# Attention's value projections held until the sixth and seventh stretch of the recurrence have gone by

## The chip, the core and the metric

The kernel runs on one NeuronCore of a Trainium2 chip. The metric is device time in microseconds (us), the median of several executions. One further execution was recorded by the hardware profiler; its trace is what is read below. Engines are named as in the profile: PE (TensorE matmul), PEld (its weight load), DVE (VectorE), ACT (ScalarE), POOL (GpSimd), SP (SyncE, which here only issues DMAs; ACT issues some too).

## The reference

Two layers are computed one after the other on 1024 tokens of width 1024. The change lies in the second one, whose token mixer runs two branches on the same normalised input and joins them:

```python
h = _rmsnorm(x, mix_norm_gain[l])
proj = h @ w_in[l]
p_rwkv, p_attn = proj[..., :RWKV_COLS], proj[..., RWKV_COLS:]
# branch 1: a recurrence over tokens, 8 heads of 64
def step(state, inp):
    r_t, w_t, k_t, v_t, kk_t, a_t = inp
    sa = jnp.einsum('bhvk,bhk->bhv', state, -kk_t)
    state = (state * w_t[:, :, None, :] + sa[..., None] * (kk_t * a_t)[:, :, None, :]
             + v_t[..., None] * k_t[:, :, None, :])
    y = jnp.einsum('bhvk,bhk->bhv', state, r_t)
    return state, y
# branch 2: causal attention, 8 heads of 64, with rotary positions on part of q and k
q, k, v = three slices of p_attn, 512 columns each
```

(The line on q, k and v stands for a few lines of the reference.) The two branches' outputs are normalised, gated, concatenated and projected; a feed-forward layer follows.

## The kernel before

**The recurrence.** The 1024 tokens are cut into 8 stretches of 128 (`NU` = 8, numbered u = 0 to 7 here; the sixth and the seventh are u = 5 and u = 6), each of 4 chunks of 32. For a stretch, `rwkv_unit` makes products on PE, then solves a triangular system in 31 steps on POOL (tiles `fs`, `Z`, `M`), after which `Z` goes through DRAM (`dz`) into the tile `xt`, of which there is one. `rwkv_maps` turns that into four maps `A` (lines 1479 and 1496, with additions on DVE). `rwkv_chain` then takes 4 steps in sequence, c0 to c3: 8 matmuls (line 1524), a multiplication on DVE that gives the next state `ST`, and a copy on ACT of the outputs into `yv`. After the fourth step `yv` goes to DRAM (`dyn`). The loop in `rwkv` runs units, maps and chains of consecutive stretches against each other.

**Attention.** `attn_in` projects q, k and v: 3 x 4 projections of 128 columns, each with its own weights of 512 KB. `weights` loads them into a tile `wraw` (two buffers), ACT rounds them to `whi`, DVE takes the rest as `wlo`; both are then used by 48 matmuls (lines 196 to 198: f32 as three products of high and low parts, 8 tiles of the contraction, two halves of the tokens). DVE scales the result into `at`, which goes to DRAM (`dqkv`). I call the four value projections V0 to V3. Below that, `attn_heads` reloads a head's q and k into tiles that share the `wraw`, `whi` and `wlo` buffers, with subtractions on POOL (`qq`, `kl`) and a fill of `qm`; `attn_max` (lines 1751 to 1759) computes a bound on the scores in 12 pairs of matmuls, each reduced on DVE, transposes it and sends it through DRAM (`dmx`) into `qm`; the scores proper (lines 1854, 1855), an exponential on ACT and a gather of values (line 1877) follow. `attn_first` does the heads and maxima of heads 0 and 1 before the attention loop; `rwkv_out` normalises the recurrence's output (`yn`, `gn`, `bon`).

**Order.** A scheduler with a timeline model sorts the instructions of all engines before the kernel is built, within what data and buffers allow; on the chip each engine takes its instructions in that fixed order. Each of SP's and ACT's DMA queues also issues in order, and each DMA waits until the eighth DMA before it, over all queues, has landed. A dependence that is added to the program can thus move instructions on all engines.

Of the kernel before, what the change touches and what calls it, by code (L numbers as in the profile page):

```python
# [17 lines left out]
P = 128  # L18
# [15 lines left out]
NU = T2 // P  # L34
# [14 lines left out]
class Build:  # L49
# [122 lines left out]
            self.ts(hi, src, 1.0, ALU.mult, eng=self.nc.gpsimd)  # L172
        self.tt(lo, src, hi.bitcast(F32), ALU.subtract, eng=lo_eng)

    def weights(self, segs, gain=None):


        kt = max(k + s.shape[0] // P for s, k, _ in segs)
        m = max(c + s.shape[1] for s, _, c in segs)
        raw = self.wp.tile([P, kt, m], F32, tag="wraw", name=self.nm("wraw"))  # L180
        for s, k, c in segs:
            self.dma(out=raw[:, k:k + s.shape[0] // P, c:c + s.shape[1]], in_=s.rearrange("(k p) m -> p k m", p=P))
        if gain is not None:
            self.tt(raw, raw, gain.unsqueeze(2).to_broadcast([P, kt, m]), ALU.mult, eng=self.nc.gpsimd)
        hi = self.wp.tile([P, kt, m], F32R, tag="whi", name=self.nm("whi"))
        lo = self.wp.tile([P, kt, m], F32R, tag="wlo", name=self.nm("wlo"))
        self.split_to(hi, lo, raw)
        return hi, lo

    def wcol(self, src, c0, m, gain=None):  # L190
        return self.weights([(src[:, c0:c0 + m], 0, 0)], gain)

    def mm3(self, ps, a, b, start, stop, **kw):

# [766 lines left out]
    def rows(self, weights, rhs, ch, acc, sink, scale, apart, between={}):  # L961


        tot = {}

        def one(j, w, ch):
            def f(ci, a, b, ps):
                src = sink(j, a, b, ps)
                if j < KD - 2:
                    self.square_acc(acc, src, j, a, b, scale)  # L970
                    return
                if a not in tot:
                    tot[a] = self.sums_ps()
                    self.add_sums(tot[a], acc[:, a:b], True, False)
                self.square_sum(tot[a], src, False, j == KD - 1, scale)

            self.proj(w, rhs, ch, f)

        end = KD - 2 if apart else KD
        for j in range(end):  # L980
            one(j, weights(j), ch)
            if j in between:
                between[j]()
        w = {j: weights(j) for j in range(end, KD)}
        res = []
        for c in ch:
            for j in w:
                one(j, w[j], [c])
            res.append(self.rstd(tot[c[0]], c[1] - c[0], D))
        return res  # L990
# [524 lines left out]
    def rwkv_chain(self, u, maps, wd):  # L1515

        nc = self.nc
        yv = self.small([P, 4, P], tag="yv", bufs=1)
        with self.tc.high_priority():
            for c in range(4):  # L1520
                S, nxt = (self.rwkv_state(4 * u + c + d) for d in range(2))
                ps = self.bank([96, 8, 64], "c0")
                for h in range(8):
                    nc.tensor.matmul(ps[:, h], maps[c][:, h], S[:, h], start=True, stop=True)
                if nxt is not None:
                    self.tt(nxt[:64].rearrange("p (q e) v -> p q e v", q=4), ps[:64].rearrange("p (q e) v -> p q e v", q=4),
                            wd[:, :, c].unsqueeze(3).to_broadcast([64, 4, 2, 64]), ALU.mult)
                nc.scalar.copy(yv[32 * c:32 * c + 32], ps[64:].rearrange("p (q e) v -> p q (e v)", q=4))
                self.rstate.pop(4 * u + c)
        self.dma(out=self.dyn[P * u:P * u + P], in_=yv)  # L1530

    def rwkv(self):

        self.xt = self.small([P, 8, P], tag="xt", bufs=1)
        self.nc.gpsimd.memset(self.xt, 0.0)
        prev = last = None
        for u in range(NU + 1):
            cur = None
            if u < NU:
                if u % 2 == 0:  # L1540
                    sl = self.lora_part(u // 2)
                cur = self.rwkv_unit(u, sl)
            if prev:
                if last:
                    self.rwkv_chain(u - 2, *last)
                last = self.rwkv_maps(prev)
            prev = cur
        self.rwkv_chain(NU - 1, *last)
# [68 lines left out]
    def attn_in(self):  # L1617
        self.dqkv = self.dram([3, 4, P, T2], "dqkv")
        for i in range(3):
            for j in range(4):  # L1620
                w = self.wcol(self.I["w_in_2"][0], 1696 + 512 * i + j * P, P)
                t = self.slot([P, T2], name="at", tag="T")
                self.proj(w, self.x, CH2, lambda ci, a, b, ps: self.tt(t[:, a:b], ps, self.rs[:, a:b], ALU.mult))
                self.dma(out=self.dqkv[i, j], in_=t)
            if i < 2:
                self.rotary(i)
# [542 lines left out]
```

## Time and profile before

| | |
|---|---|
| median of 3 runs | 3237.48 us (3234.71 to 3238.14) |
| the profiled execution | 3233.1 us |
| its span in the trace | 3231.4 us |
| PE busy | 93% of the span |
| DVE, POOL, ACT busy | 62%, 41%, 35% |
| mean granted PE clock | 0.941 |

[...] Times in the rows below are counted from the start of the span.

### The profile page before, as it was taken

How to read it: one execution, taken by the hardware profiler on the slowest of the kernel's cores; microseconds unless marked ns; L12 is line 12 of the kernel's file. 1: busy time of each engine (PE TensorE's matmuls, PEld its weight loads, DVE VectorE, ACT ScalarE, POOL GpSimd, SP SyncE). 2: the span in 40 equal slices, each digit the busy share in tenths (PEclk: the TensorE clock that was granted, in tenths of full speed). 3: DMA queues.
4: the chain of work that ended last, by engine and by line, in shares of the span. 5: the costliest groups of instructions: out<-in, count | busy, mean ns of one | idle time of the engine just before them, and what ended most of it. 6: DMA issues, size and time to landing. Idle time of an engine off the chain costs nothing.

```text
span 3231.4 us, 52682 instructions
## 1 busy us (share of the span) xinstructions
PE 3009.3 (93%) x20614; PEld 2678.5 (83%) x20614; DVE 2009.6 (62%) x3618; ACT 1142.4 (35%) x2168; POOL 1335.0 (41%) x1291
## 2 busy tenths in 40 slices
PE   7999999989799999999999988788988899999998
PEld 6999998979799999877877776677778788887777
DVE  7556654674676666466776555558656766664666
ACT  3344313334343333311333323424444333334111
POOL 3767310033654444232532365543214744454430
PEclk9999999989799999999899989858998899999999
DMA  5333532335222222432223554533425122224321
GB/s 148 86 94 111 174 98 59 105 101 139 78 66 79 81 82 81 150 104 74 90 95 131 146 126 112 137 99 108 115 98 196 53 85 79 80 83 174 113 85 53
DMA packets 322535, 336.83 MB, mean 104 GB/s; under 512 B 60081, under 2 KB 270734, under 8 KB 322286
## 3 DMA queue, kind: packets, MB, share of 16 engines
q1 hardware_dynamic: 289646, 310.38, 31.0%
q10 hardware_dynamic: 32640, 23.08, 2.3%
q8 instruction: 162, 2.65, 0.3%
q14 instruction: 87, 0.71, 0.1%
HBM read 232.66 MB, written 96.40 MB: 102 GB/s over the span
## 4 chain that ended last, share of the span: by engine, by line
PE 61%; DVE 11%; POOL 7%; issue 5%; DMA 4%; ACT 2%; SPq 2%; ACTq 0%; DVEq 0%; POOLq 0%
PE pm L196 13%; PE pm L197 12%; PE pm L198 12%; PE px L197 5%; PE px L196 5%; PE px L198 5%; POOL fs L149 2%; POOL Z L149 2%; DVE dn L149 2%; SPq L142 2%; PE px L292 1%; DVE t L149 1%; PE pa L1877 1%; DMA M<-dm 1%; PE pc L1604 1%
## 5 line engine op out<-in xcount | busy, mean ns | idle before, releaser
L196 PE MATMUL pm<-xh,whi 128*128 128x512 f32 (+5 forms) x1344 | 446.9, 333 | 14.2 <-DVE th L149 11.5
L198 PE MATMUL pm<-xh,wlo 128*128 128x512 f32 (+5 forms) x1344 | 446.8, 333 | 0.0
L197 PE MATMUL pm<-xl,whi 128*128 128x512 f32 (+5 forms) x1344 | 446.4, 332 | 0.0
L149 DVE TENSOR_TENSOR y<-y,pm 128x512 f32<-128x512 f32 (+1 forms) x336 | 218.1, 659 | 159.4 <-PE pm L198 159.1
L196 PE MATMUL pm<-dn,dn 128*128 128x512 f32 (+1 forms) x736 | 286.0, 389 | 6.5 <-DVE y L149 6.2
L196 PEld LDWEIGHTS pm<-xh,whi 128*128 128x128 f32 (+1 forms) x1344 | 257.8, 192 | 35.8 <-DVE th L149 12.4
L197 PE MATMUL pm<-dn,dn 128*128 128x512 f32 (+1 forms) x736 | 282.4, 384 | 1.3 <-POOL dn L149 1.3
L198 PE MATMUL pm<-dn,dn 128*128 128x512 f32 (+1 forms) x736 | 282.5, 384 | 0.0
L197 PEld LDWEIGHTS pm<-xl,whi 128*128 128x128 f32 (+1 forms) x1344 | 257.6, 192 | 19.7 <-issue 0.9
L198 PEld LDWEIGHTS pm<-xh,wlo 128*128 128x128 f32 (+1 forms) x1344 | 257.8, 192 | 19.1 <-issue 0.5
L149 POOL TENSOR_TENSOR dn<-hid,dn 128x1024 fp32r<-128x1024 f32 x44 | 131.8, 3012 | 250.9 <-ACT dn L1161 250.9
L197 PE MATMUL px<-t,sh 128*128 128x258 f32 (+2 forms) x684 | 218.7, 320 | 6.9 <-DVE t L149 6.8
L196 PE MATMUL px<-t,sh 128*128 128x258 f32 (+2 forms) x684 | 217.2, 318 | 0.4 <-DVE gt L149 0.3
L198 PE MATMUL px<-t,sl 128*128 128x258 f32 (+2 forms) x684 | 216.1, 316 | 0.0
L149 DVE TENSOR_TENSOR wlo<-wraw,whi 128x1024 fp32r<-128x1024 f32 (+2 forms) x114 | 153.9, 1351 | 76.2 <-ACT whi L170 74.7
L196 PEld LDWEIGHTS pm<-dn,dn 128*128 128x128 f32 x736 | 138.2, 188 | 43.7 <-DVE y L149 14.2
L170 ACT CAST whi<-wraw 128x1024 fp32r<-128x1024 f32 (+2 forms) x114 | 103.4, 908 | 185.7 <-PE pm L197 154.8
L197 PEld LDWEIGHTS pm<-dn,dn 128*128 128x128 f32 x736 | 138.4, 188 | 29.9 <-POOL dn L149 1.7
L198 PEld LDWEIGHTS pm<-dn,dn 128*128 128x128 f32 x736 | 138.2, 188 | 30.0
L170 ACT CAST dn<-wd 128x1024 fp32r<-128x1024 f32 x44 | 46.1, 1048 | 290.8 <-PE pm L197 290.3
L197 PEld LDWEIGHTS px<-t,sh 128*128 128x128 f32 x684 | 131.3, 192 | 17.9 <-DVE t L149 9.1
L149 POOL TENSOR_TENSOR wraw<-wraw,par 128x1024 f32<-128x1024 f32 (+1 forms) x36 | 73.4, 2041 | 169.0 <-DMA wraw<-in_w_in_dram 128.7
(600 smaller groups left out, 8788.6 us busy)
## 6 DMA issues: line engine op xcount, KB each, us to landing
wraw<-in_w_in_dram SPq DMA_DIRECT2D x61, 512.0 KB
dhid<-up SPq DMA_DIRECT2D x44, 512.0 KB
wd<-in_w_ffn_down_dram SPq DMA_DIRECT2D x44, 512.0 KB
hid<-dhid SPq DMA_DIRECT2D x44, 512.0 KB
wra<-in_w_ffn_up_dram SPq DMA_DIRECT2D x33, 512.0 KB
wrb<-in_w_ffn_up_dram SPq DMA_DIRECT2D x33, 512.0 KB
dg<-th SPq DMA_DIRECT2D x16, 514.0 KB
wraw<-in_w_out_dram SPq DMA_DIRECT2D x16, 512.0 KB
```

The costliest lines, as they stand in the source:

```text
L142: self.nc.sync.dma_start(out=out, in_=in_)
L149: (eng or self.nc.vector).tensor_tensor(out=o, in0=a, in1=b, op=op)
L170: self.nc.scalar.copy(hi, src)
L196: nc.tensor.matmul(ps, a[0], b[0], start=start, stop=False, **kw)
L197: nc.tensor.matmul(ps, a[0], b[1], start=False, stop=False, **kw)
L198: nc.tensor.matmul(ps, a[1], b[0], start=False, stop=stop, **kw)
L292: self.nc.tensor.matmul(ps[:bw, i:i + 1], src[:, i * bw:i * bw + bw], self.ones[:, 0:1], start=start and i == 0, stop=stop and i == n - 1)
L1604: nc.tensor.matmul(ps, w[:, k], (yh, yl, yh)[q][:, a:b], start=i == 0, stop=i == 11)
L1877: nc.tensor.matmul(self.po[:, i - 4 * ch], pT[:, i * P - a:i * P - a + P], self.vx[j % 2][:, k].rearrange("p e v -> p (e v)")[:, 2 * e:2 * ...
```

## The change

At the end of each stretch's chain one column of `yv` is copied into a small tile `held[u]` (8 copies of 128 x 1 on DVE). Before the weights of a value projection are loaded, one column of the buffer they go to is written from such a tile: from `held[5]` for V0 and V1, from `held[6]` for V2 and V3 (4 copies of 128 x 1 on DVE). The load overwrites that column, so the numbers computed are the same; what is new is that the load must follow the copy. Nothing is taken out.

```diff
-    def weights(self, segs, gain=None):
+    def weights(self, segs, gain=None, hold=None):
...
         raw = self.wp.tile([P, kt, m], F32, tag="wraw", name=self.nm("wraw"))
+        if hold is not None:
+            self.nc.vector.tensor_copy(raw[:, 0, :1], hold)
         for s, k, c in segs:
             self.dma(out=raw[:, k:k + s.shape[0] // P, c:c + s.shape[1]], in_=s.rearrange("(k p) m -> p k m", p=P))
...
         self.dma(out=self.dyn[P * u:P * u + P], in_=yv)
+        self.held[u] = self.small([P, 1], tag="held", bufs=3)
+        nc.vector.tensor_copy(self.held[u], yv[:, 0, :1])
...
-                w = self.wcol(self.I["w_in_2"][0], 1696 + 512 * i + j * P, P)
+                w = self.wcol(self.I["w_in_2"][0], 1696 + 512 * i + j * P, P, hold=self.held[NU - 3 + j // 2] if i == 2 else None)
```

The scheduler moves much with it. On SP's queue, before, the loads of value weights stood among the transfers of the third to fifth stretch; here is the one of V3 (`wraw_22143`), behind the fifth stretch's `M` and ahead of the loads of q and k for the rotation (`ro`).

```order
L142 DMA dm_19426<-pr_19332 32x8x32 x4
L142 DMA ST_19693<-dvn_16713 32x512
L142 DMA M_19557<-dm_19426 32x1024 x4
L142 DMA ST_19706<-dvn_16713 32x512
L142 DMA A_19769<-KT_18910 32x768 x2
L142 DMA dqkv_21408<-at_21872 128x1024
L142 DMA wraw_22143<-in_w_in_dram 128x8x128
L142 DMA ro_21926<-dqkv_21408 16x8x128
```

After, on the same queue, V0's and V1's loads (`wraw_21979`, `wraw_22040`) stand behind the solved system of the seventh stretch (`dz_20618`, `xt`), the last stretch's `M` and the sixth stretch's output (`dyn`).

```order
L142 DMA dz_20618<-Z_20519 256x1x32 x2
L142 DMA M_20986<-dm_20855 32x1024 x4
L142 DMA xt_17610<-dz_20618 32x8x32 x4
L142 DMA A_21200<-KT_20346 32x768 x2
L142 DMA ST_21234<-dvn_16713 32x512
L142 DMA yn_22343<-dyn_16712 128x2x256
L142 DMA ST_21247<-dvn_16713 32x512
L142 DMA dyn_16712<-yv_21095 128x512
L142 DMA wraw_21979<-in_w_in_dram 128x8x128
L142 DMA wraw_22040<-in_w_in_dram 128x8x128
```

V2's and V3's loads stand behind the `dyn` of the seventh stretch, and the loads of q and k of heads 0 and 1 (`raw`) behind those, so four large loads have moved past the transfers of three or four stretches. On PE, before, V3's last matmuls are followed by the first matmul of head 0's maxima and by maps (line 1496) of the sixth stretch: the maxima stand inside the recurrence's last three stretches.

```order
L196 MATMUL pm_3008_22176<-xh_16212,whi_22145 128x512
L197 MATMUL pm_3008_22176<-xl_16213,whi_22145 128x512
L198 MATMUL pm_3008_22176<-xh_16212,wlo_22146 128x512
L1751 MATMUL pm_3023_22232<-kk_22218,qq_22217 128x256
L1496 MATMUL pm_2815_20694<-LR_19858 96x96
L1496 MATMUL pc_2816_20695<-LR_19858 96x96
```

After (line numbers are up to 5 higher), V3 is followed by the same maxima, but all maps and all chain steps, the last stretch's too, stand ahead of it; the first score (line 1859, `pm_3140`) has been put between, while the matmul that completes it stands behind all maxima of head 0.

```order
L198 MATMUL pm_3016_22196<-xh_16212,whi_22165 128x512
L199 MATMUL pm_3016_22196<-xl_16213,whi_22165 128x512
L200 MATMUL pm_3016_22196<-xh_16212,wlo_22166 128x512
L1756 MATMUL pm_3031_22252<-kk_22238,qq_22237 128x256
L1785 MATMUL pq_3041_22289<-ident_66,vT_22263 128x128 x4
L1859 MATMUL pm_3140_22697<-qq_22237,kk_22238 128x512
L1757 MATMUL pm_3031_22252<-kl_22223,qm_22226 128x256
```

V0 and V1 stand after the loads of the seventh stretch's `xt` and among its maps and its steps c0 and c1; then come the last stretch's `xt` product, the steps c2 and c3 of the seventh stretch and c0 and c1 of the eighth, and only behind these V2 (with c2 and c3 of the eighth stretch inside it) and V3. On POOL, the subtractions and fills of heads 0 and 1, which stood inside the seventh solve, stand behind the eighth.

## Rows read from the trace of the kernel before

**Rows 1.** The page: the chain that ended last, share of the span by engine.

```profile
PE 61%; DVE 11%; POOL 7%; issue 5%; DMA 4%; ACT 2%; SPq 2%; ACTq 0%; DVEq 0%; POOLq 0%
```

**Rows 2.** Windows: length, busy of PE, PEld, DVE, ACT, POOL, then granted clock.

```profile
2070.00:2100.00 30.00, 19.57 (x329) 16.58 (x329) 16.35 (x34) 15.88 (x29) 18.57 (x51) 0.90 0.60 160
2100.00:2130.00 30.00, 22.70 (x202) 21.03 (x203) 12.90 (x34) 6.05 (x13) 16.85 (x41) 0.61 0.36 86
2130.00:2160.00 30.00, 30.00 (x346) 25.87 (x345) 19.10 (x61) 9.64 (x22) 15.44 (x46) 0.50 0.33 95
2160.00:2190.00 30.00, 26.75 (x159) 23.99 (x159) 21.38 (x66) 8.57 (x16) 4.96 (x6) 0.50 0.35 112
2190.00:2230.00 40.00, 33.28 (x174) 29.11 (x174) 37.42 (x111) 16.91 (x35) 14.45 (x13) 0.76 0.33 99
```

**Rows 3.** Who PE waited for, 2000 to 2200 us.

```profile
PE pm L1752 <- POOL qm L1735: 11.3, 1, 11.3
```

**Rows 4.** Timeline of POOL: the solves of the sixth to eighth stretch.

```profile
2036.27 0.24 POOL L149 TENSOR_TENSOR fs<-Z,M 128x31 f32<-128x31 f32 x1 [11.28 <-DMA M<-dm]
...
2061.94 0.22 POOL L149 TENSOR_TENSOR Z<-Z,fs 128x8 f32<-128x8 f32 x1
...
2079.03 0.24 POOL L149 TENSOR_TENSOR fs<-Z,M 128x31 f32<-128x31 f32 x1 [8.00 <-DMA M<-dm]
...
2085.55 2.63 POOL L149 TENSOR_TENSOR kl<-raw,kk 64x1024 fp32r<-64x1024 f32 x1
...
2111.99 0.21 POOL L149 TENSOR_TENSOR Z<-Z,fs 128x8 f32<-128x8 f32 x1
2122.47 0.24 POOL L149 TENSOR_TENSOR fs<-Z,M 128x31 f32<-128x31 f32 x1 [10.26 <-DMA M<-dm]
```

**Rows 5.** Timeline of SP's queue after the seventh solve.

```profile
2112.56 2.56 SPq L142 DMA_DIRECT2D dz<-Z  x4
...
2119.73 0.92 SPq L142 DMA_DIRECT2D xt<-dz  x2
...
2129.76 6.30 SPq L142 DMA_DIRECT2D ST<-dvn  x2
```

**Rows 6.** Chain that ended last, in order of time: start, us, what.

```profile
2080.98 1.50 PE pc L1524 x16
...
2122.73 1.99 PE pm L1479 x8
...
2164.96 2.82 PE pc L1524 x16
```

**Rows 7.** The same chain where a weight load stood open.

```profile
1515.24 5.05 DMA wraw<-in_w_in_dram
```

**Rows 8.** Tile whi, 1900 to 2000 us: casts and splits of weights (ns min/median/max).

```profile
L170 ACT CAST whi<-wraw x3: 1044/1048/1056, 1925.6 to 1982.9; 128x1024 fp32r<-128x1024 f32 x3
L149 DVE TENSOR_TENSOR wlo<-wraw,whi x3: 1206/1210/1227, 1928.1 to 1985.5; 128x1024 fp32r<-128x1024 f32 x3
```

**Rows 9.** Timeline of PE inside a projection.

```profile
2013.50 0.40 PE L196 MATMUL pm<-xh,whi 128*128 128x512 f32 x1
2013.73 0.39 PE L197 MATMUL pm<-xl,whi 128*128 128x512 f32 x1
```

**Rows 10.** Line 1753, 2085 to 2160 us: the maxima of head 0 (ns).

```profile
L1753 DVE CUSTOM_DVE_ANT_0 pm<-pm,mask x8: 299/566/700, 2101.6 to 2141.7; 128x384 f32<-128x384 f32 x2, 128x512 f32<-128x512 f32 x2, 128x128 f32<-128x128 f32 x1, 128x256 f32<-128x256 f32 x1
...
L1753 DVE CUSTOM_DVE_ANT_0 pm<-pm,mask,mx x4: 560/658/758, 2113.7 to 2146.8; 128x320 f32<-128x320 f32 x1, 128x384 f32<-128x384 f32 x1, 128x448 f32<-128x448 f32 x1, 128x512 f32<-128x512 f32 x1
```

**Rows 11.** Timeline of PE: transpose of the maxima.

```profile
2150.57 0.38 PE L1759 MATMUL pm<-ident,mx 128*8 128x128 f32 x1
```

**Rows 12.** Timeline of SP's queue: the maxima's way back.

```profile
2158.72 0.39 SPq L142 DMA_DIRECT2D qm<-dmx  x1
```

**Rows 13.** Timeline of PE: the first score's second half.

```profile
2189.25 0.63 PE L1855 MATMUL pm<-qm,kl 66*128 66x512 f32 x1
```

**Rows 14.** Line 1572: the nearest tiny copies on DVE (ns).

```profile
L1572 DVE COPY bon<-yn x16: 136/144/153, 2138.7 to 2241.2; 128x1 f32<-128x1 f32 x16
```

More of the change, by code (lines that the diff above doesn't have):

```diff
@@ L188, in weights, with wcol @@
         return hi, lo
-    def wcol(self, src, c0, m, gain=None):
-        return self.weights([(src[:, c0:c0 + m], 0, 0)], gain)
+    def wcol(self, src, c0, m, gain=None, hold=None):
+        return self.weights([(src[:, c0:c0 + m], 0, 0)], gain, hold)
     def mm3(self, ps, a, b, start, stop, **kw):
@@ L1536, in rwkv @@
         prev = last = None
+        self.held = {}
         for u in range(NU + 1):
```

## The prediction

> **What bounds the kernel now.** I read the chain of the work that ended last first: PE holds 61% of it, DVE 11%, POOL 7% [rows 1]. Over the whole span, then, matmuls are the limit, but the change touches one short stretch that can be limited otherwise, so next come windows of it [rows 2]. From 2070 to 2100 us PE is busy only 19.57 of 30 us. From 2100 on it looks full (30.00 of 30 us in 2130 to 2160), but the granted clock there is 0.50: at full speed the same matmuls would fill half. The list of waits says what stood ahead of that: a matmul of head 0's maxima waited 11.3 us for the fill of `qm` on POOL [rows 3], and POOL was inside the seventh solve.
>
> POOL's timeline gives the beat of the recurrence. The sixth solve runs from 2036.27 to 2062.16, 25.9 us. The seventh runs from 2079.03 to 2112.20, 33.2 us, because attention's heads (such as `kl`, 2.63 us) stand inside it. The eighth starts at 2122.47. Ahead of each, POOL stands idle for `M`: 11.28, 8.00 and 10.26 us [rows 4]. From the end of the seventh solve, SP issues `dz` and `xt`, and PE can start the next maps 10.5 us later, at 2122.73 [rows 5, 6]. So in this stretch it is a round trip from POOL through SP and DRAM to PE that paces the work, and PE has room. Before the change V0 to V3 fill that room early; by 2188 us everything that attention needs is there, and the first score is complete from 2189.25 [rows 13]. I take that matmul as the finish line of the stretch: behind it, by the order of DVE and PE, about as much is left to do after the change as before.
>
> **What the change costs.**
>
> *Twelve small copies.* The nearest are of the same shape, 144 ns each [rows 14]: 1.7 us in all, on a DVE that is busy 12.90 of 30 us where most of them stand [rows 2]. Nothing at best, 1.7 us if all lay on the path; I take nothing, and this stays far below the other terms.
>
> *The matmuls that move.* V0 to V3 are 192 matmuls of 128 x 512. Two in a row start 0.23 us apart at full clock [rows 9]: 44.7 us, that leave a stretch which is paced by POOL and stand behind the seventh solve. The casts and splits that go with them (1.05 us on ACT, 1.21 us on DVE each [rows 8]) and the scalings of the outputs overlap them, except where a wait below counts them.
>
> *PE's work from the seventh solve to the finish line, if it never waited.* I price it from the windows at full clock [rows 2]: 2122.7 to 2130 is 7.3 x 0.61 = 4.4 us, 2130 to 2160 is 30.00 x 0.50 = 15.0, 2160 to 2189 is about 28.7/30 of 26.75 x 0.50 = 12.8; together 32.2 us. With V it is 77 us. The seventh solve, free of the heads' operations, should take what the sixth took: it ends at 2079.0 + 25.9 = 2104.9, and PE can start 10.5 us later, at 2115.4. Without any wait the finish line would be at 2192.4, 3.2 us later than now.
>
> *The waits that the new order makes.* (a) The loads of V0 and V1 stand on SP behind the seventh stretch's `xt`, whose last transfer is now issued 8.5 us after the solve, and behind six or seven more issues. At 0.4 to 0.6 us each that puts the load at about 2117; a single `ST` issue can hold the queue for some 3 us (two took 6.30 [rows 5]), so I take 2119. One weight load that the chain stood open for took 5.05 us [rows 7]; with cast and split, V0's matmuls start at 2126.5. PE has only the product with `xt`, about 2 us, to do before: 9 us of waiting. [...] (c) The chain's steps around V2's arrival: a step's 16 records take 1.50 us of PE [rows 6], but each waits for the multiplication on DVE that makes its state. For four steps without projections between them I take 1 us each, 4 us. (d) V2's load waits for the last step of the seventh stretch: copy of `yv`, small copies, issue, 5.05 us, cast and split make 8.5 us, of which two steps and maps of the last stretch cover half: 4 us. (e) Head 0's maxima now stand together behind V3. Their reductions take 8 x 0.566 + 4 x 0.658 = 7.2 us on DVE [rows 10], paced by DVE instead of being spread over three stretches: 4 us beyond the PE work already counted. (f) Then come the transpose, the way through DRAM into `qm`, and only then the matmul that completes the first score. Now transpose to issue of the last transfer is 2150.57 to 2158.72 [rows 11, 12], 8.2 us, with some 2 us to land; a part of it was DVE and SP busy with other things, so I take 9 us, with no other work of size for PE. Today this trip is hidden under 30 us of recurrence, which is the cover that is lost. Sum: 9 + 3 + 4 + 4 + 4 + 9 = 33 us.
>
> *What comes back.* With V out of the way, products and chains of the fourth to sixth stretch run earlier, and the waits for `M` before the sixth and seventh solve (11.28 and 8.00 us) can shrink. Nothing if SP's and DRAM's latencies make them, some 16 us if 3 us of waiting remain; POOL and SP being the same as before, I take 7 us, below the middle. After 2190, where the clock is 0.76 on average [rows 2], DVE is busy 37.42 of 40 us and would be the limit at any clock; I take 1 us.
>
> Sum: +3.2 + 33 - 7 - 1 = +28 us. Against the profiled execution's own 3233.1 us (span 3231.4) that is 3261; the median of the runs shown lies 4.4 us above that execution, and I add the sum to the median: 3265.5, say 3265 us, slower by 0.85%.
>
> [...] The rows: PE's clock falls to 0.50 behind a wait of 11.3 us and stays there for some 90 us, in which PE's records are short groups of small matmuls [rows 2, 3]. [...]
>
> **Rivals.** *No change.* The waits (a) to (f) find cover that my reading of the order misses, and only the sum of PE's work is left: the clock gives back 34 us (66 us of tail against 32 of work at full rate) for the 44.7 that come in, the solve 7 us, and the end moves by 3.2 us: about 3241. For it speaks that PE is at 0.50 for so long now; against it that (a), (d) and (f) are round trips in a fixed order. *Faster.* The recurrence's beat falls: its products and chains no longer stand behind projections on PE, so that `M` arrives for the sixth and seventh solve with 3 us of waiting, and the seventh ends 16 us earlier than in my sum's start. The place to see it is POOL's idle time ahead of these two solves. Without waits the finish line would be at 2192.4 - 16 = 2176, 13 us earlier than now, 3224 in all; an earlier beat also widens the cover for (a) and (d), since SP's queue would run ahead. It decides where 16 us exceed 3.2 plus the waits that are left: these would have to shrink from 33 to under 13 us, to under 6 for a gain of 0.2%. For it speaks that V0 to V3 do stand among these stretches now, against it that 25.9 + 10.5 us of the beat are not PE's at all. *Much slower.* The clock stays low for V2 and V3, because the chain's waits come just before them: their 96 matmuls cost about twice, +20 us, and with a few us more for the loads the end is near 3290. For it speaks how long the clock stayed at 0.50 after one wait. That the hold does not bind can be left out: by the order, V3's load stood ahead of the sixth solve's transfers and now follows the seventh stretch's last step.
>
> **Chances.** My forecast, 3250 to 3280: 0.60. Between that and no change: 0.06. Much slower: 0.14. No change (within 0.2%, 6.5 us, about what a measurement of this kernel can tell): 0.10. Faster: 0.10. For the range I leave out the last two but for their edge and the end of the slow case: 3242 to 3290. Slower by over 0.2% gets 0.60 + 0.06 + 0.14 = 0.80.
>
> **What would show it.** Right: the last two solves end by about 2105 and 2143; the granted clock falls before 2115 and rises within V0; waits for the cast or split of V0's and V2's weights of some 9 and 4 us appear on PE; the maxima of head 0 stand behind V3, and a wait of some 9 us for `qm` stands ahead of the second half of the first score, at about 2217. Wrong: solves that come much earlier (the beat), a clock of 0.50 through V2 and V3, or a finish line that moves while the end of the kernel does not, because DVE or a later wait takes the shift up.

## The result, and the profile after

The changed kernel takes 3275.43 us (median of 4 runs, 3271.49 to 3284.16), the kernel before, beside it, 3236.18 us: a ratio of 1.0122, 95% interval 1.0108 to 1.0136. It is slower by 39 us, where 28 were forecast. The profiled execution of the changed kernel took 3284.16 us (span 3282.4), the slowest of its four, against 3233.1 (span 3231.4) before; so this pair of traces differs by 51 us, 12 more than the medians do, and what is read from the two must not be added up to 39. One execution of only_second_pair below (3400.72 us) and one of the kernel before beside the short_v and yn_act runs (3677.24 us) ran at a granted clock of 0.81 and 0.73 in place of 0.93 to 0.94, and ratios and medians leave them out.

A part of the 51 us has nothing to do with the change. Up to the first solve of the second layer, PE and SP take the same instructions in the same order in both traces, yet that solve starts 3.8 us later in the trace after. POOL's timeline before and after:

```profile
1831.86 0.24 POOL L149 TENSOR_TENSOR fs<-Z,M 128x31 f32<-128x31 f32 x1 [32.63 <-DMA M<-dm]
```

```profile
1835.62 0.24 POOL L149 TENSOR_TENSOR fs<-Z,M 128x31 f32<-128x31 f32 x1 [32.23 <-DMA M<-dm]
```

To compare times of two traces I therefore also count from this solve.

First the windows of the trace after, which answer to [rows 2]. The columns are length, busy time and count of PE, PEld, DVE, ACT and POOL, then granted clock, DMA share and GB/s.

```profile
2010.00:2040.00 30.00, 21.80 (x295) 19.41 (x296) 8.36 (x14) 5.76 (x13) 10.85 (x31) 0.57 0.38 82
2040.00:2070.00 30.00, 23.19 (x282) 19.88 (x269) 17.41 (x42) 12.28 (x30) 20.59 (x62) 0.54 0.25 67
2070.00:2100.00 30.00, 22.17 (x374) 19.71 (x375) 14.50 (x38) 6.73 (x15) 16.24 (x46) 0.61 0.36 90
2100.00:2130.00 30.00, 17.13 (x268) 14.69 (x268) 9.22 (x32) 7.78 (x18) 16.86 (x57) 0.50 0.32 81
2130.00:2160.00 30.00, 29.05 (x192) 23.66 (x192) 10.83 (x17) 6.84 (x13) 9.74 (x28) 0.98 0.37 102
2160.00:2190.00 30.00, 29.25 (x192) 25.00 (x190) 17.01 (x44) 7.03 (x10) 1.04 (x1) 0.72 0.54 147
2190.00:2220.00 30.00, 25.67 (x122) 19.99 (x120) 11.61 (x25) 12.24 (x17) 14.34 (x12) 0.94 0.34 103
2220.00:2250.00 30.00, 22.93 (x98) 16.89 (x98) 26.72 (x96) 7.74 (x17) 7.16 (x9) 0.72 0.29 82
```

From 2010 to 2130 us, where V0 to V3 have left, PE runs at 0.50 to 0.61. From 2130 to 2160 V0 and V1 fill it at 0.98, where before it had been at 0.50. So the clock did come up in the tail, and the kernel still became slower. What grew stands behind the recurrence. The timeline of PE there: the last matmuls of V3, the first of head 0's maxima, the transpose of the maxima, and the matmul that completes the first score.

```profile
2210.29 0.40 PE L198 MATMUL pm<-xh,whi 128*128 128x512 f32 x1
...
2210.99 0.28 PE L1756 MATMUL pm<-kk,qq 128*128 128x256 f32 x1
...
2226.80 0.38 PE L1764 MATMUL pm<-ident,mx 128*8 128x128 f32 x1 [0.66 <-DVE mx L1758]
...
2231.48 0.80 PE L1860 MATMUL pm<-qm,kl 66*128 66x512 f32 x1 [1.16 <-DMA qm<-dmx]
```

V3 ends just ahead of 2210.99; from there to the transpose the 12 pairs of maxima take 15.8 us, and the way through DRAM another 4.7. The first score is complete from 2231.48, 42.2 us later than 2189.25 in [rows 13], or 38.5 us when both are counted from the first solve. ACT's timeline has the arrival of V2's weights (the cast) and the copy of the very last step's output:

```profile
2170.14 0.58 ACT L1530 COPY yv<-pc 32x512 f32<-32x512 f32 x1 [0.72 <-DVE ST L149]
...
2179.78 1.04 ACT L170 CAST whi<-wraw 128x1024 fp32r<-128x1024 f32 x1 [3.45 <-DMA wraw<-in_w_in_dram]
...
2197.68 0.58 ACT L1530 COPY yv<-pc 32x512 f32<-32x512 f32 x1 [6.12 <-PE pc L1526]
```

That last copy started at 2194.70 in the trace before. So the recurrence itself ends 3 us later, and counted from the first solve 0.8 us earlier: it is not what became late. Before, the first score was complete 5.4 us ahead of it, and now it is 33.8 us behind. Of the 51 us between the two profiled executions, 3.8 were there before the first solve, 38.5 arise up to the first score, the attention loop accounts for 6 (its last gather of values starts at 2457.3 after, 2408.9 before, 48.4 us apart) and the rest of the kernel for 3.

### The profile page after: what moved, and what is told of

It reads as the page before. It is cut to its first block, busy times and chain, and to the rows that moved or that the text cites. A ratio compares the mean times of both kernels' runs of the same rounds, so it can differ in the third digit from the quotient of the medians.

```text
span 3282.4 us, 52687 instructions
## 1 busy us (share of the span) xinstructions
PE 3035.2 (92%) x20614; PEld 2697.4 (82%) x20614; DVE 2014.1 (61%) x3630; ACT 1142.5 (35%) x2168; POOL 1343.6 (41%) x1291
## 4 chain that ended last, share of the span: by engine, by line
PE 61%; DVE 10%; POOL 6%; issue 5%; DMA 4%; ACT 2%; SPq 2%; ACTq 0%; DVEq 0%; POOLq 0%
PE pm L198 13%; PE pm L199 13%; PE pm L200 13%; PE px L199 5%; PE px L198 5%; PE px L200 5%; POOL Z L149 2%; POOL fs L149 2%; SPq L142 2%; DVE dn L149 2%; PE px L294 2%; DVE t L149 1%; PE pa L1882 1%; DMA M<-dm 1%; DVE y L149 1%
```

## The experiments

Every one of these kernels is sorted anew by the scheduler, so an edit can move more than it names; the orders on PE are told where they matter. For each I give the ratio to the kernel before on the same chip, and three readings of its trace: the start of the layer's first solve, of the last copy of the recurrence's output, and of the matmul that completes the first score (1831.86, 2194.70 and 2189.25 before, 1835.62, 2197.68 and 2231.48 after). By the intervals, a difference between two of these ratios is known to 6 to 12 us, and the prices below with it.

| run | ratio (95% interval) | median, before beside it | first solve | last copy | first score |
|---|---|---|---|---|---|
| copies_no_wait | 0.9981 (0.9967 to 0.9994) | 3235.22, 3241.9 | 1834.12 | 2195.02 | 2189.43 |
| two_earlier | 1.0023 (1.0011 to 1.0035) | 3249.44, 3241.9 | 1833.66 | 2188.04 | 2195.49 |
| all_on_fourth | 1.0054 (1.0038 to 1.0071) | 3253.95, 3235.1 | 1831.25 | 2200.70 | 2201.13 |
| all_on_sixth | 1.0071 (1.0056 to 1.0086) | 3267.22, 3241.9 | 1832.63 | 2200.13 | 2215.91 |
| only_second_pair | 1.0064 (1.0041 to 1.0088) | 3264.49, 3241.9 | 1830.11 | 2186.72 | 2217.96 |
| heads_held | 1.0064 (1.0046 to 1.0082) | 3259.4, 3239.67 | 1832.20 | 2204.99 | 2222.18 |
| one_later | 1.0145 (1.0126 to 1.0165) | 3286.49, 3239.67 | 1833.26 | 2186.20 | 2240.75 |
| short_v_before | 0.9937 (0.9919 to 0.9956) | 3219.53, 3239.71 | 1832.49 | 2180.15 | 2175.06 |
| short_v_after | 1.0019 (1.0003 to 1.0035) | 3245.62, 3239.71 | 1836.85 | 2196.30 | 2209.92 |
| yn_act_after | 1.0130 (1.0100 to 1.0160) | 3281.51, 3239.71 | 1828.44 | 2192.92 | 2227.16 |
| yn_act_before | 1.0016 (1.0003 to 1.0029) | 3244.84, 3239.71 | 1833.70 | 2196.24 | 2190.22 |
| heads_dve_before | 1.0036 (1.0023 to 1.0049) | 3251.16, 3239.67 | 1831.58 | 2206.45 | 2201.36 |

My theory was that the loss is set by what the new order puts behind the recurrence (projections, maxima, their way through DRAM) and by waits for weights. The rivals: the copies, the disturbed middle stretches with their low clock, and single stalls such as one of DVE.

**copies_no_wait: the copies, without a wait.**

```diff
-                w = self.wcol(self.I["w_in_2"][0], 1696 + 512 * i + j * P, P, hold=self.held[NU - 3 + j // 2] if i == 2 else None)
+                w = self.wcol(self.I["w_in_2"][0], 1696 + 512 * i + j * P, P, hold=self.sgn if i == 2 else None)
```

> All 12 small copies stay, but the column of the weight buffer is written from a constant that was ready long ago, so no load has to wait for a stretch. By my theory (the cost is the place of the value projections and the waits around them) this is the kernel before within 3 us: about 3237. By the rival that the copies themselves, on a busy DVE, cost something: 3240 or more; if half the loss were theirs, 3255.

PE's order is that of the kernel before, and so is the first score, 0.2 us apart. Twelve small copies cost nothing that can be measured; the time is even 0.19% below, some 6 us, which I cannot explain.

**two_earlier: the hold two stretches earlier.**

```diff
-        self.held[u] = self.small([P, 1], tag="held", bufs=3)
+        self.held[u] = self.small([P, 1], tag="held", bufs=8)
...
-                w = self.wcol(self.I["w_in_2"][0], 1696 + 512 * i + j * P, P, hold=self.held[NU - 3 + j // 2] if i == 2 else None)
+                w = self.wcol(self.I["w_in_2"][0], 1696 + 512 * i + j * P, P, hold=self.held[NU - 5 + j // 2] if i == 2 else None)
```

> The same hold, two stretches earlier: V0 and V1 wait for the fourth stretch, V2 and V3 for the fifth. By my theory the hold costs only where the projections and head 0's maxima no longer find recurrence to lie under; here V3 ends among the last two stretches and the maxima stand among the last stretch's steps, so most of the 39 us should be gone: 3236 to 3250. By the rival that any hold of this kind upsets the order and empties PE in the middle stretches (low clock, slower chain): 3260 or more, near the changed kernel's 3275.

0.23% above the kernel before, some 7 us. PE's order has V3 behind the seventh stretch's maps and the maxima among the last steps. The first score, from PE's timeline:

```profile
2195.49 0.78 PE L1860 MATMUL pm<-qm,kl 66*128 66x512 f32 x1
```

This hold costs little; where it lets the projections lie matters more than that there is one. It is not the whole rule: all_on_fourth below, with an early hold too, loses more.

**all_on_sixth: V0 and V1 held as in the change, V2 and V3 without a wait of their own.**

```diff
-                w = self.wcol(self.I["w_in_2"][0], 1696 + 512 * i + j * P, P, hold=self.held[NU - 3 + j // 2] if i == 2 else None)
+                w = self.wcol(self.I["w_in_2"][0], 1696 + 512 * i + j * P, P, hold=self.held[NU - 3] if i == 2 and j < 2 else None)
```

> V0 and V1 wait for the sixth stretch as in the change; V2 and V3 have no wait of their own and follow when the two weight buffers come free. The wait for V2's weights (about 8 us from the end of the seventh stretch's chain) goes, and V2 and V3 lie among the last stretch's steps. By my theory 15 to 25 us come back: 3250 to 3260. By the rival that the stall of DVE ahead of the sixth stretch's last step (12.4 us for a load of the output normalisation, seen in the trace after) is what costs: it is still there, so little comes back: 3268 to 3276.

0.71% above before where the change was 1.22%: some 16 us came off, within what the theory said, and the first score is 15.6 us earlier than after the change, though the last step is 2.5 us later:

```profile
2215.91 0.77 PE L1860 MATMUL pm<-qm,kl 66*128 66x512 f32 x1
```

So V2's and V3's wait for the seventh stretch, and the matmuls that it puts behind the last step, are worth about 16 of the 39 us, or 10 to 23 by the intervals.

**only_second_pair: V0 and V1 free, V2 and V3 held.**

```diff
-                w = self.wcol(self.I["w_in_2"][0], 1696 + 512 * i + j * P, P, hold=self.held[NU - 3 + j // 2] if i == 2 else None)
+                w = self.wcol(self.I["w_in_2"][0], 1696 + 512 * i + j * P, P, hold=self.held[NU - 2] if i == 2 and j > 1 else None)
```

> V0 and V1 are free as before the change; V2 and V3 wait for the seventh stretch. Half of the matmuls that moved go back under the recurrence; but V2 and V3, head 0's maxima and their way through DRAM still stand behind the last stretch. By my theory what stands behind the last chain sets the end: V3 ends where the seventh stretch's chain allows, so some 15 us come back from V0 and V1, not 30: 3255 to 3265. By the rival that V0's and V1's place (and the stall ahead of them) costs most: below 3250.

0.64% above before, some 21 us, the edge of what was expected; of the loss, some 19 us go with V0 and V1. These prices are not parts of one sum: each edit gives a new order, and what is taken out with one pair may also be covered in another way. The last step is 11 us earlier than after the change, the first score 13.5 us.

**short_v_before and short_v_after: most of V's matmuls left out.** One tile of the contraction instead of eight in V0 to V3, in either kernel.

```diff
-                self.proj(w, self.x, CH2, lambda ci, a, b, ps: self.tt(t[:, a:b], ps, self.rs[:, a:b], ALU.mult))
+                self.proj(w, self.x if i < 2 else self.x[:1], CH2, lambda ci, a, b, ps: self.tt(t[:, a:b], ps, self.rs[:, a:b], ALU.mult))
```

> The kernel before, with V0 to V3 summing over one of the eight tiles of the contraction only: 24 of their 192 matmuls are left, 39 us of matmuls at full clock are left out (the values of attention are not the right ones then). By my theory V lies under waits of the recurrence in the kernel before, so hardly anything is gained: 0 to 8 us. By the rival that PE's work sets the time there too, as 61% of the chain says, the gain is 25 us or more.

> The changed kernel with the same 168 matmuls left out. By my theory the moved matmuls stand uncovered and most of their 39 us come off: 20 to 35 us less than the changed kernel, that is some 12 us above the kernel before, for the waits that are left. By the rival that the waits for weights and the way of the maxima through DRAM are the whole loss, less than 10 us come off.

Neither reading of the kernel before held: 20 us came off, between the two. The first score of either, before and after:

```profile
2175.06 0.63 PE L1855 MATMUL pm<-qm,kl 66*128 66x512 f32 x1
```

```profile
2209.92 0.79 PE L1860 MATMUL pm<-qm,kl 66*128 66x512 f32 x1 [4.27 <-DMA qm<-dmx]
```

V did not lie wholly under waits of the recurrence: of 39 us of matmuls about half were on the path already. The difference that the change makes shrinks from 1.22% to 0.82% (1.0019 over 0.9937), from 39 to 26 us. So with hardly any matmul left to move, two thirds of the loss stay; by the intervals of the two ratios these are 18 to 34 us. I take them as order and waits, the weights among them, which are still loaded in full: in the short kernel too the last step ends at 2196.30, and maxima and their way end 13.6 us behind it. What the theory had expected of the changed kernel (20 to 35 us off) came out, 30 to 34 us; what it said of the kernel before did not. The first score moves by 30.5 us between the two short kernels, counted from the first solve, where the time moves by 26.

**yn_act_after and yn_act_before: the loads of the output normalisation on ACT's queue.**

```diff
-        self.dma(out=yn, in_=self.dyn[t0:t0 + NT, 2 * g:2 * g + 2, :].rearrange("(t p) q v -> p t q v", p=P))
+        self.store(out=yn, in_=self.dyn[t0:t0 + NT, 2 * g:2 * g + 2, :].rearrange("(t p) q v -> p t q v", p=P))
```

> The changed kernel with the loads of the output normalisation issued from ACT's queue instead of SP's, where they stand behind the transfers of the last two solves. If the 12.4 us in which DVE stood still for the first of them, with the sixth stretch's last step behind it, are on the path, 6 to 12 us come off; if V0's weights or the solve would have been late anyway, nothing, or it gets worse because ACT's queue is in order too.

> The same edit of the kernel before, as a control. The chain that ended last passed through five of these loads in the last 80 us of the recurrence, 11% of that stretch; but the loads wait for the chain's outputs, not for SP: within 4 us of the kernel before.

In the trace after the change DVE stood still for one of these loads with the chain behind it. DVE's timeline: the reduction at 2121.33 waited 12.42 us for the load, and the multiplication `ST` of the sixth stretch's last step stands behind it.

```profile
2108.22 0.69 DVE L149 TENSOR_TENSOR pr<-pq,pr 128x512 f32<-128x512 f32 x1 [1.13 <-PE pq L1448]
2121.33 0.69 DVE L1565 TENSOR_REDUCE gn<-yn 128x8 f32<-128x512 f32 x1 [12.42 <-DMA yn<-dyn]
...
2124.31 0.67 DVE L149 TENSOR_TENSOR ST<-pc,wd 64x512 f32<-64x512 f32 x1
```

With the loads on the other queue that wait is gone, but another took its place: DVE now waited 12.91 us for POOL's part of the same normalisation, and PE waited 12.3 us where it had waited 12.9. The first score came 4.3 us earlier, but this trace was 7.2 us ahead at the first solve already (1828.44 beside 1835.62), so counted from there it came 2.9 us later. V0's load was issued at 2118.52, counted in the same way only 1.3 us earlier: what it waits for now stood behind POOL, which does this part of the normalisation inside the eighth solve.

```profile
2116.29 0.22 DVE L1577 COPY bon<-yn 128x1 f32<-128x1 f32 x2 [12.91 <-POOL yn L149]
```

```profile
2227.16 0.79 PE L1860 MATMUL pm<-qm,kl 66*128 66x512 f32 x1 [3.17 <-DMA qm<-dmx]
```

The time did not fall (1.0130, interval 1.0100 to 1.0160, beside 1.0122); by the intervals a gain of over 8 us is excluded. The stall is real, but the load on SP's queue does not by itself explain the loss. That the stall costs nothing is not shown, since one of the same length took its place. The control, the same edit of the kernel before, came out 5 us above it (1.0016), just outside the 4 us expected.

**heads_held: only head 0's maxima held.** Projections are free; the reload of q and k for head 0 waits for the seventh stretch.

```diff
-                w = self.wcol(self.I["w_in_2"][0], 1696 + 512 * i + j * P, P, hold=self.held[NU - 3 + j // 2] if i == 2 else None)
+                w = self.wcol(self.I["w_in_2"][0], 1696 + 512 * i + j * P, P, hold=None)
...
+        if h == 0:
+            for raw in raws:
+                nc.vector.tensor_copy(raw[:, :1], self.held[NU - 2])
```

> V0 to V3 are free as before the change; instead the reload of head 0's q and k (not the values) waits for the seventh stretch's outputs, by the same small copies. So only head 0's maxima and their way through DRAM move behind the last steps, with all projections done early. In the trace after, the 12 pairs of maxima took 15.8 us and the way to the first score 4.7 us, behind a recurrence that ended at the same time within 3 us. By my theory these come back to 10 to 18 us here, as a few pairs lie under the last steps: 3250 to 3258 beside 3240. By the rival that the moved matmuls and their weights are the whole loss: below 3246.

0.64%, some 20 us, a little more than expected: holding the maxima back, with the order that this brings, costs half of what the change lost, with all projections done early. PE's timeline, the transpose of the maxima and the first score, with a wait of 4.88 us for `qm`:

```profile
2214.97 0.38 PE L1767 MATMUL pm<-ident,mx 128*8 128x128 f32 x1 [1.46 <-DVE gn L153]
...
2222.18 0.80 PE L1863 MATMUL pm<-qm,kl 66*128 66x512 f32 x1 [4.88 <-DMA qm<-dmx]
```

It is not the price of the maxima alone. With no projections in the tail the clock was at 0.50 from 2100 to 2220 throughout (before, it is 0.76 on average from 2190 on [rows 2]), and the last step was 10 us later than before, so the recurrence is in it too. Here the first score is 33 us later than before and the time only 20: the reading is not a measure to the microsecond.

```profile
2130.00:2160.00 30.00, 20.43 (x168) 18.03 (x158) 10.33 (x27) 5.70 (x12) 11.22 (x35) 0.50 0.33 91
...
2190.00:2220.00 30.00, 21.14 (x81) 15.56 (x79) 27.63 (x85) 8.67 (x16) 11.18 (x10) 0.50 0.44 122
```

**one_later: the hold one stretch later.**

```diff
-                w = self.wcol(self.I["w_in_2"][0], 1696 + 512 * i + j * P, P, hold=self.held[NU - 3 + j // 2] if i == 2 else None)
+                w = self.wcol(self.I["w_in_2"][0], 1696 + 512 * i + j * P, P, hold=self.held[NU - 2 + j // 2] if i == 2 else None)
```

> The hold one stretch later: V0 and V1 wait for the seventh, V2 and V3 for the eighth stretch. By my theory what stands behind the last step sets the time: 132 matmuls or 31 us instead of 58 or 13 us, and V2's load after the last step adds a wait of some 5 us beyond V1's cover: 20 to 25 us above the changed kernel, 3298 to 3304 beside 3240. By the rival that the changed kernel loses by its disturbed middle stretches, no more than 8 us above it.

1.45%, only some 8 us above the change (0 to 15 by the intervals), where I had 20 to 25. ACT's timeline and PE's show where they went.

```profile
2186.20 0.58 ACT L1530 COPY yv<-pc 32x512 f32<-32x512 f32 x1 [6.09 <-PE pc L1526]
```

```profile
2217.08 0.28 PE L1756 MATMUL pm<-kk,qq 128*128 128x256 f32 x1
...
2234.41 0.38 PE L1764 MATMUL pm<-ident,mx 128*8 128x128 f32 x1 [0.91 <-DVE gn L153]
...
2240.75 0.79 PE L1860 MATMUL pm<-qm,kl 66*128 66x512 f32 x1 [4.31 <-DMA qm<-dmx]
```

The last step's copy is at 2186.20, 11.5 us earlier than after the change, as V0 and V1 no longer stand among the steps; V3 ends 6 us later, and maxima and way take 23.7 us instead of 20.5. I had counted the matmuls that go behind the last step and not what their leaving gives back. By its number (no more than 8 us above) the rival came out, but not by its reason: the middle stretches are as empty here, and the recurrence ends 8.5 us earlier than before the change, not later.

**heads_dve_before: heads 0 and 1 off POOL, in the kernel before.** The two subtractions and the fill go to DVE for these heads.

```diff
-        self.tt(qq[64:], raws[0][64:], qq[64:].bitcast(F32), ALU.subtract, eng=pool)
+        self.tt(qq[64:], raws[0][64:], qq[64:].bitcast(F32), ALU.subtract, eng=pool if h > 1 else None)
...
-        self.tt(kl[:64], raws[1][:64], kk[:64].bitcast(F32), ALU.subtract, eng=pool)
+        self.tt(kl[:64], raws[1][:64], kk[:64].bitcast(F32), ALU.subtract, eng=pool if h > 1 else None)
...
-        pool.memset(qm[64:66].bitcast(F32), 0.0)
+        (pool if h > 1 else nc.vector).memset(qm[64:66].bitcast(F32), 0.0)
```

> The kernel before, with the subtractions and fills of heads 0 and 1 on DVE instead of POOL, where they stood inside the seventh solve and PE waited 11.3 us for one of them. By my theory the end of the recurrence is paced by the solves and their round trips: the seventh solve is some 7 us shorter, and 4 to 8 us come off: 3230 to 3236 beside 3240. If DVE or the loads are late next, nothing comes off.

It is slower, 0.36%. The seventh solve is shorter, as meant (27.8 us instead of 33.2), but the eighth starts 2.3 us later than in [rows 4]: it waited 18.82 us for `M`.

```profile
2078.08 0.24 POOL L149 TENSOR_TENSOR fs<-Z,M 128x31 f32<-128x31 f32 x1 [10.95 <-DMA M<-dm]
...
2105.69 0.21 POOL L149 TENSOR_TENSOR Z<-Z,fs 128x8 f32<-128x8 f32 x1
2124.72 0.24 POOL L149 TENSOR_TENSOR fs<-Z,M 128x31 f32<-128x31 f32 x1 [18.82 <-DMA M<-dm]
```

A shorter solve does not bring the next one forward when `M` is late for another reason; which of DVE's and SP's waits made it late I have not separated. So the beat that the prediction read, solve and round trip, is not alone in setting the end of the recurrence.

**all_on_fourth: V0 and V1 held to the fourth stretch, V2 and V3 without a wait of their own.** The edit of all_on_sixth with `NU - 5` for `NU - 3`, and eight buffers of `held`.

> V0 and V1 wait for the fourth stretch, V2 and V3 have no wait of their own. Beside the run in which V2 and V3 waited for the fifth stretch (7.5 us above the kernel before), only their wait is gone; the same edit two stretches later took 14 to 16 us off. By my theory there is less to gain here, since all projections and most maxima already lie under the recurrence: 0 to 6 us off, 3236 to 3243 beside 3240. By the rival that a second wait for weights costs the same wherever it stands: 3230 or less, faster than before.

0.54%, slower than two_earlier by some 10 us, against both expectations. Taking V2's own wait away two stretches earlier did not help; the last step is 12.7 us later than in two_earlier. Why the order came out so much worse is open: here my theory of what lies behind the last step does not explain the 18 us. No kernel of this study with the full computation is faster than the kernel before by over 0.2%.

## Why the prediction was right, and where its terms were off

**Right:** slower, and in the range. The finish line that was chosen, the first complete score, ranks the runs nearly as their times do; the clear exceptions are heads_held (33 us later, 20 us in time) and short_v_after (21 and 6). After the change it moved by 42.2 us, 38.5 counted from the first solve, where the sum said 28. Nearly all of that miss lies ahead of V0. PE's timeline has its first matmul:

```profile
2132.26 0.50 PE L198 MATMUL pm<-xh,whi 128*128 128x512 f32 x1 [0.88 <-ACT whi L170]
```

With its 7 us of "what comes back" taken off, the sum has V0 at 2119.5 and the first score 98 us behind that. Measured are 2132.26 (2128.5 on the count of the trace before) and 99.2 us. That the second part fits so well is luck in part: inside it (b), (c), (d), (e) and (f) are off in both directions.

**The solves.** POOL's timeline, to be set beside [rows 4]: starts and ends of the sixth to eighth solve.

```profile
2041.72 0.24 POOL L149 TENSOR_TENSOR fs<-Z,M 128x31 f32<-128x31 f32 x1 [14.01 <-DMA M<-dm]
...
2066.88 0.21 POOL L149 TENSOR_TENSOR Z<-Z,fs 128x8 f32<-128x8 f32 x1
...
2081.36 0.24 POOL L149 TENSOR_TENSOR fs<-Z,M 128x31 f32<-128x31 f32 x1 [9.31 <-DMA M<-dm]
...
2107.09 0.21 POOL L149 TENSOR_TENSOR Z<-Z,fs 128x8 f32<-128x8 f32 x1
2116.27 0.24 POOL L149 TENSOR_TENSOR fs<-Z,M 128x31 f32<-128x31 f32 x1 [8.97 <-DMA M<-dm]
```

The seventh took 25.9 us, as forecast from the sixth. But it started at 2081.36, 2.3 us later than before, or 1.4 us earlier counted from the first solve, where the term "what comes back" had it 7 us earlier. (The forecast's own sign, solves that end by about 2105 and 2143, leaves these 7 us out; it came, with 2107.30 and 2141.92.) POOL still waited 14.01 us ahead of the sixth and 9.31 ahead of the seventh. So the step that failed is the sentence that the waits for `M` shrink once V has left PE. With V's matmuls left out of the kernel before they do shrink, in short_v_before:

```profile
2027.86 0.24 POOL L149 TENSOR_TENSOR fs<-Z,M 128x31 f32<-128x31 f32 x1 [7.37 <-DMA M<-dm]
...
2076.43 0.24 POOL L149 TENSOR_TENSOR fs<-Z,M 128x31 f32<-128x31 f32 x1 [3.56 <-DMA M<-dm]
```

In the changed kernel V's matmuls have left this stretch as well, and the waits are longer than in [rows 4]; with those matmuls left out there too (short_v_after) they are 18.21 and 9.77 us. So it is not V's share of PE that keeps `M` late after the change, and what differs is the order. On SP's queue the transfer `dm`, from which `M` is read, is issued 13.2 us behind the fifth solve's `dz` after the change (2019.68 to 2032.90), 10.8 us before it and 3.3 us in short_v_before, since other transfers and what they wait for stand between. Which of them decides is open. (In either trace no more than eight DMAs, of both queues together, were under way at any time.)

**(a) V0's weights.** Forecast: issue at 2119, V0 at 2126.5. The chain that ended last, after the change, goes from the seventh solve through SP's issues to the load of `yn` whose wait stands above, then through DVE to the loads of V0's and later of V2's weights (start, us, what):

```profile
2117.06 0.52 SPq L142
2117.68 3.62 DMA yn<-dyn
...
2124.31 0.67 DVE ST L149
...
2127.02 4.07 DMA wraw<-in_w_in_dram
...
2172.74 7.02 DMA wraw<-in_w_in_dram
```

From the end of the solve (2107.30) SP's issues take 10.4 us up to that of `yn`; the forecast gave SP's queue 14 us up to V0's load, so its size was right. What it did not have is the load of `yn` and the step behind it on DVE, 9.3 us more: V0's load was issued at 2127.02, 8 us late. PE's list of waits shows what this did to PE:

```profile
PE pq L1438 <- DVE KT L149: 17.0, 3, 12.9
```

12.9 us for a result of DVE (`KT`, products of the last stretch, behind the same stall), only 0.9 us for the weights. So the maps began 20.3 us behind the seventh solve (2107.30 to 2127.55), where the sum had 10.5. The forecast wait of 9 us was there in size, but in front of the maps instead of behind them, and its releaser was another: that it came out near is luck.

**(b) The 3 us at V0's start,** a term of the sum for a V0 that begins at half clock: no run shows it. The granted clock was 0.50 up to 2130, rose in the next window, under the products with `xt`, and was at 1.00 from 2132 on, when V0 started:

```profile
2130.00:2132.00 2.00, 1.38 (x8) 1.13 (x7) 0.00 (x0) 0.84 (x1) 1.55 (x5) 0.73 1.19 305
```

Half clock stood at V2's start instead: its first matmul starts at 2180.87, and from 2175 to 2185 the clock is 0.50. V0 and V1 ran at 0.98 (2130 to 2160), and the sparse stretches that V left at 0.50 to 0.61 (2010 to 2130). The clock told little of the time, since its gain in the tail was less than what the order lost. One reading of the prediction was also wrong: before the change the clock did not stay at 0.50 for some 90 us behind the wait of 11.3 us. It was back at 0.98 from 2112 to 2118, fell again when PE waited 6.4 us for a load of `ST`, and was at 0.50 from 2118 to 2198.

**(c), (d) V2's weights.** From the copy of the seventh stretch's last output (2170.14) to the issue of the load it is 2.6 us, to the cast 9.6 us, of which 7.0 are the landing, where [rows 7] had 5.05. So V2's first matmul came 10.7 us behind that copy, some 2 us more than the 8.5 us of (d). The forecast sign, a wait of PE for these weights, did not appear, since PE had steps and maps to do, at a granted clock of 0.50 from 2175 on; but the chain above runs through this load and its cast, so it was on the path, as forecast. all_on_sixth prices this hold, together with the matmuls that it puts behind the last step, at some 16 us; (c) and (d) were 8.

**(e) The maxima.** 15.8 us where I had 7.2 us of reductions and 4 of exposed time. DVE had the output normalisation's instructions between the reductions, and two of these were held up (last section); the granted clock was 0.94 up to 2220 and 0.72 behind it. **(f) The way through DRAM** took 4.7 us, not 9; of it 1.6 us lie between the issue of the last transfer (2229.85) and the first score, where I had some 2 us to land (a load of `ST` in the chain of before landed in 1.98 us, at 2120.76). Together 20.5 instead of 16 us behind V3, counting PE's work in (e).

**The work term, +3.2 us.** By the short kernels the moved matmuls make 13 of the 39 us, known to some 9, and all the rest 26. The forecast had the moved matmuls nearly free: it set 44.7 us against a clock that gives 34 back and a shorter solve, so it counted the tail at full clock, and the clock was 0.72 in two of its four windows. The 26 us contain the waits and what did not come back, so they are not to be held against the forecast's 33 us of waits alone; with what comes back (7 and 1) taken off, those were 25. That the two are so near does not show the parts to be right, and (a) to (f) above show that they were not. The premise that V lies in room that PE has anyway held for only half of V: 20 of its 39 us were on the path before the change.

So the direction and the kind of loss were right: the order puts waits and the maxima behind the recurrence, and the clock's gain does not pay for it. The term that failed is what comes back (-7, measured between -1.4 and +2.3); the work term and the way in which the waits divide were mis-sized. What stays open is how the 26 us divide between PE's 12.9 us wait, the loads and the maxima: taking one stall away gave another.

**The rivals.** No change and faster fell: the waits for `M` did not shrink and the waits found no cover. Much slower, by a low clock in V2 and V3, fell as a time; the windows of V2 and V3 are at 0.72 and 0.94, so its condition held for the start of V2 only.

## What to carry to other kernels

Before work is moved behind a recurrence, look at what else must wait for it there: here the 45 us of matmuls cost some 13 of the 39 us, while holding back only the maxima, which with their transpose and way through DRAM had been hidden under the last steps, cost some 20. A stretch that reads as paced by waits can still hold half of a filler's time on the path: leave the filler out once and measure, rather than call it covered. And where a scheduler sorts the program, a dependence is priced by the order that comes out, on all queues: here a load behind another stretch's transfers held a step of the recurrence for 12 us, though neither had anything to do with the values; and two edits that looked alike, two_earlier and all_on_fourth, came out 10 us apart.

## What the runs showed of the hardware

Two instructions of DVE on 128 x 8 elements, which take 0.15 to 0.17 us in the rows around them, took 2.00 and 2.09 us among the maxima. POOL's timeline shows what ran beside them, and DVE's the reductions that came next to them:

```profile
2215.74 2.00 DVE L149 TENSOR_TENSOR gn<-gn 128x8 f32<-128x8 f32 x1
2217.66 0.49 DVE L1758 CUSTOM_DVE_ANT_0 pm<-pm,mask 128x320 f32<-128x320 f32 x1
...
2218.07 2.09 DVE L156 SCALAR_TENSOR_TENSOR gn<-gn,gn 128x8 f32<-128x8 f32 x1
```

```profile
2215.36 2.35 POOL L149 TENSOR_TENSOR qq<-raw,qq 64x1024 fp32r<-64x1024 f32 x1 [0.76 <-DMA raw<-dqkv]
2217.79 2.34 POOL L149 TENSOR_TENSOR kl<-raw,kk 64x1024 fp32r<-64x1024 f32 x1
```

Both ended within 0.04 us of the end of a subtraction on POOL (2215.36 + 2.35 = 2217.71 and 2217.79 + 2.34 = 2220.13). The reductions of the maxima from 2213 to 2225, of 256 to 512 columns, took 0.42 to 0.70 us, the one between the two 0.49. So each of the two `gn` instructions ended only with the POOL instruction beside it, some 1.9 us late, 3.8 us in all between reductions that the first score waits for; why is not shown. It is no effect of the change: in the trace before, beside the same two subtractions for another head (2215.10 + 2.37 = 2217.47 and 2218.44 + 2.35 = 2220.79), two such instructions took 2.02 and 2.06 us and ended 0.02 us behind them.

```profile
2215.47 2.02 DVE L156 SCALAR_TENSOR_TENSOR gn<-gn,gn 128x8 f32<-128x8 f32 x1
...
2218.00 0.17 DVE L149 TENSOR_TENSOR gn<-gn 128x8 f32<-128x8 f32 x1
...
2218.75 2.06 DVE L156 SCALAR_TENSOR_TENSOR gn<-gn,gn 128x8 f32<-128x8 f32 x1
```

The one at 2218.00 ran beside POOL's fill of `qm` (2217.41 + 0.95 us) and took 0.17 us, so it was not held.
